# Two weight tiles at a time in layer two's dense products, and five layouts of split weight tiles

## The chip, the core and the metric

The kernel runs on one core of a Trainium2 chip. Its time is the device time of one execution in microseconds (us). TensorE multiplies, VectorE and ScalarE do elementwise work, GpSimd a little of it, and SyncE issues the transfers from HBM to the on-chip memory SBUF. In the profile these engines are PE (matrix products), PEld (the loads of PE's stationary operand, which overlap the products), DVE, ACT, POOL and SP. Three runs of the kernel before gave a median of 2337.14 us (2336.44 to 2337.54).

## The reference

The program is two layers of an encoder. A layer projects the residual stream with one wide matrix, runs gated linear attention and neighbourhood attention, projects back, adds and normalises, and then runs a squared-ReLU MLP with another normalisation:

```python
for l in range(DEPTH):                                   # DEPTH = 2
    proj = h @ w_in[l]                                   # 2048 -> 6176 columns
    mix  = concat(gla(proj), na(proj)) @ w_out[l]        # 2048 -> 2048
    h    = layer_norm(ALPHA * h + mix)
    ff   = square(relu(h @ w_ff1[l])) @ w_ff2[l]         # 2048 -> 8192 -> 2048
    h    = layer_norm(ALPHA * h + ff)
return h[:, 16:]                                         # the 16 meta tokens are dropped
```

There are 272 positions: 256 tokens and 16 meta tokens. Everything is float32. In layer two the meta tokens' results are needed only as keys and values, so most of that layer's products have 256 columns and not 272.

## The kernel before

**Three products for one.** Activations and weights are held as a high part and a low part (`x = h + l`, `w = wh + wl`, each in the type float32r), and a product is the sum of `wh*h`, `wh*l` and `wl*h`. A weight tile of 128 partitions x 1024 columns holds eight stationary blocks of 128x128. SP fetches it as `raw` (L189), ACT casts it to the high part `wh` (L212), DVE subtracts to get the low part `wl` (L213). `raw`, `wh` and `wl` have three buffers each, so a tile may be split when the tile three before it is used up.

**The layout of a split tile.** `wh` and `wl` are 1280 columns wide, so the eight blocks need not lie side by side. `blocks` takes three numbers: where the first block lies, how far the second block of a pair lies behind the first, and how far the next pair lies behind this one. Before, two sets of numbers exist: one for tiles whose products run in the short form below (high: 24, P, 2P; low: 8, P+32, 2P+64, with P = 128), and one for all the others (high: 0, P, 2P; low: 0, P+16, 2P+64). All numbers are float32 columns, 4 bytes each.

**The products of a tile.** `by_m` makes one output tile of 128 rows after another; each sums over `nk` blocks, eight to a weight tile, and calls `eight` for each weight tile. `eight` (its product is L247) issues PE's products in an order that a string gives: `h` is high weights times high activations, `l` high weights times low activations, `w` low weights times high activations. The long form, `hlhlww...`, has 24 products of up to 274 columns. The short form, `hwhw...`, is used where a product has 256 columns: the high and the low part of an activation lie close enough for one `h` product of 512 columns to do `wh*h` and `wh*l`, into the two halves of a PSUM bank; `w` is a product of 256 columns into the second half. An evict adds the halves.

**Dense and pitched activations.** In a dense activation tile the two parts of 256 columns lie side by side, and an `h` product streams 512 columns in one piece. The attention's outputs `y` and the MLP's inner activations `u` of layer two are dense, and so is `x` after layer two's first normalisation. Where `x` still has 272 positions (layer two's first projection) the parts are 288 columns apart, so that `h` streams two pieces of 256; these are called pitched here.

**What runs when.** Layer one uses the long form with 272 columns throughout. Where the normalisation is still being finished, the first two groups of a matrix run with two columns more (274 in layer one's MLP and in layer two's first projection, 258 in layer two's MLP), so that a product also gives two sums that the late correction needs. Layer two's short-form products are: 20 output tiles pitched in the first projection, then dense 12 output tiles of the output projection, 52 of the MLP's first matrix, and 31 of 32 of its second (whose `nk` is 32). `by_k` (L273) does the first group of some matrices, four output tiles at once.

**What sets the order.** Each engine takes its instructions in the order of its list. The lists follow the order in which the code issues, apart from a few places where the framework moves a product ahead because it expects another one's operand to be late. `weights` keeps one split tile ahead of the one in use; `pump` lets background generators (normalisation, attention) issue a step between tiles.

Of the kernel before, what the change touches and what calls it, by code (L numbers as in the profile page):

```python
# [14 lines left out]
P = 128  # L15
D = 2048
DC = D // P
T = 256
# [8 lines left out]
WB = 1024  # L27
# [11 lines left out]
PAD = 40  # L39
PITCH = 288  # L40
WIDE = 1280
HIGHS = {True: 24, False: 0}
LOWS = {True: (8, P + 32, 2 * P + 64), False: (0, P + 16, 2 * P + 64)}
TURNS = {True: "hwhwhwhwhwhwhwhw", False: "hlhlwwhlhlwwhlhlwwhlhlww"}


class Pair(tuple):


    def __new__(cls, both, dense=False):  # L50
        flat = both.rearrange("p a c -> p (a c)")
        parts = (flat[:, :T], flat[:, T:2 * T]) if dense else (both[:, 0, :], both[:, 1, :])
        made = super().__new__(cls, parts)
        made.both, made.once = both, flat[:, :2 * T] if dense else both[:, :, :T]
        return made


class Trunk:
    def __init__(self, ctx, tc, ins, out):
        self.ctx, self.tc, self.nc = ctx, tc, tc.nc  # L60
        self.i, self.out = ins, out
        self.bg, self.fg, self.credit, self.fcredit = deque(), deque(), 0, 0
        self.wants, self.due, self.late = {}, None, 0
        self.x = [None] * DC
        self.stream, self.ready = self.order(), deque()
        pool = lambda name, **k: ctx.enter_context(tc.tile_pool(name=name, **k))
        self.cp = pool("const", bufs=1)
        self.xp = pool("xhl", bufs=1)
        self.yp = pool("yhl", bufs=1)
        self.wp = pool("wst", bufs=3)  # L70
        self.jp = pool("jn", bufs=1)
        self.pm = pool("pm", bufs=4, space=PSUM)
        self.pb = pool("pb", bufs=4, space=PSUM)
# [80 lines left out]
    def order(self):  # L154

        i, first = self.i, [(), (WB // 2, WB)]
        for l in range(DEPTH):
            last = l + 1 == DEPTH
            na = [last and c % 3 == 0 for c in range(24)]
            groups = [(i["win"][l, g], [last and g in (3, 4, 5)] * 4 if g < 6 else na[4 * g - 24:4 * g - 20]) for g in range(12)]  # L160
            groups += [(i["wout"][l, g], [last and g > 0] * 4) for g in range(4)]
            for half in range(2):
                groups += [(i["wff1"][l, 8 * half + g], [last and (half > 0 or g > 2)] * 4) for g in range(8)]
                groups += [(i["wff2"][l, half, g], [last] * 4) for g in range(4)]
            if l == 0:
                for t in range(groups[0][0].shape[0]):
                    for w, _ in groups[:2]:
                        yield w[t], first.pop(0) if first else (WB,), False
                groups = groups[2:]
            for w, once in groups:  # L170
                n = w.shape[0]
                for t in range(n):
                    yield w[t], (WB,), once[4 * t // n]

    def weights(self):

        while len(self.ready) < 2:
            self.ready.append(self.made(*next(self.stream, (None, (), False))))
        return self.ready.popleft()

    def made(self, ap, ends, once):
        if ap is None:
            return None
        nc = self.nc
        raw = self.wp.tile([P, WB], F32, name="raw", tag="raw")
        wh, wl = (self.wp.tile([P, WIDE], F32R, name=nm, tag=nm) for nm in ("wh", "wl"))
        wh, wl = self.blocks(wh, HIGHS[once], P, 2 * P), self.blocks(wl, *LOWS[once])
        for c in map(slice, (0,) + ends, ends):
            nc.sync.dma_start(raw[:, c], ap[:, c])  # L189
            self.halves(raw[:, c], wh, wl, slice(c.start // P, c.stop // P))  # L190
        if not ends:
            self.head(ap, raw, wh, wl)
        return wh, wl
# [21 lines left out]
    def head(self, ap, raw, wh, wl):  # L215

        nc, q = self.nc, WB // 4
        both = self.xr.tile([P, 2, q + L], F32, name="head", tag="head", bufs=1)
        self.x[:2] = [self.pair(self.xp, "x", c) for c in range(2)]
        for c in range(2):  # L220
            nc.sync.dma_start(both[:, c], self.i["head"][:, c])
        nc.sync.dma_start(raw[:, 2 * q:], ap[:, 2 * q:])
        for c in range(2):
            at = slice(2 * c, 2 * c + 2)
            h, lo = (t[:, :L] for t in self.x[c])
            acts = lambda: self.split(both[:, c, q:], h, lo)
            weights = lambda: self.halves(both[:, c, :q], wh, wl, at)
            for f in (weights, acts) if c else (acts, weights):
                f()
        for at in (slice(4, 6), slice(6, 8)):  # L230
            self.halves(raw[:, at.start * P:at.stop * P], wh, wl, at)

    def eight(self, ps, wh, wl, x, n, first, last, once):
# [6 lines left out]
        for i, kind in enumerate(TURNS[once]):  # L240
# [5 lines left out]
                rhs, o = (v.once, ps) if kind == "h" else (v[0][:, :T], ps[:, T:])  # L246
            mm(o, lhsT=self.block(w, j), rhs=rhs, start=first and not i, stop=last and i == len(TURNS[once]) - 1)  # L247

    def whole(self, parts):

        if len(parts) == 1:
            return parts[0]
        t = self.jp.tile([P, T], F32, name="jn", tag="jn")
        self.nc.scalar.copy(t, parts[1])
        self.nc.vector.tensor_tensor(t, t, parts[0], ALU.add)
        return t
# [20 lines left out]
    def by_m(self, acts, ns, evict, pump=(0, 0), apart=False, renew=False, slim=()):  # L277

        nk = len(acts)
        for m, n in enumerate(ns):  # L280
            once = n == T and m not in slim
            ps = self.pm.tile([P, 512], F32, name="mm", tag="mm")
            for k in range(0, nk, 8):
                wh, wl = self.weights()
                self.eight(ps, wh, wl, acts[k:k + 8], n, not k, k == nk - 8, once)
                if k < nk - 8:
                    self.pump(*pump)
                if renew and m == len(ns) - 1 and not k:
                    self.renew(2)
            parts = [ps[:, :T], ps[:, T:]] if once else [ps[:, :n]]  # L290
            evict(m, parts if apart else self.whole(parts))
            self.pump(*pump)
# [916 lines left out]
```

## Time and profile before

| what | us |
|---|---|
| median of three runs | 2337.14 |
| the profiled execution | 2336.72 |
| its span, first to last instruction | 2334.9 |
| PE busy | 2326.3 |
| PEld busy (overlaps PE) | 2216.0 |
| DVE busy | 1527.4 |
| ACT busy | 1211.8 |
| POOL busy | 129.4 |

The profiled execution takes 1.8 us more than its span. PE is busy almost all the time, at a granted clock of 0.999. The traffic is 419 MB, nearly all of it the weights. A row of the timeline gives the start and the recorded duration of an instruction, or of several equal ones that follow each other; a product's recorded duration is longer than the time until the next product starts, because products are pipelined.

### The profile page before, as it was taken

How to read it: one execution, taken by the hardware profiler on the slowest of the kernel's cores; microseconds unless marked ns; L12 is line 12 of the kernel's file. 1: busy time of each engine (PE TensorE's matmuls, PEld its weight loads, DVE VectorE, ACT ScalarE, POOL GpSimd, SP SyncE). 2: the span in 40 equal slices, each digit the busy share in tenths (PEclk: the TensorE clock that was granted, in tenths of full speed). 3: DMA queues.
4: the chain of work that ended last, by engine and by line, in shares of the span. 5: the costliest groups of instructions: out<-in, count | busy, mean ns of one | idle time of the engine just before them, and what ended most of it. 6: DMA issues, size and time to landing. Idle time of an engine off the chain costs nothing.

```text
span 2334.9 us, 44618 instructions
## 1 busy us (share of the span) xinstructions
PE 2326.3 (100%) x18180; PEld 2216.0 (95%) x18180; DVE 1527.4 (65%) x2432; ACT 1211.8 (52%) x2100; POOL 129.4 (6%) x200
## 2 busy tenths in 40 slices
PE   9999999999999999999999999999999999999998
PEld 9999999999999999999999899989988888888888
DVE  5588777775544455546576887778766555666655
ACT  5666664564433344444456666655654334445443
POOL 0021110110000000000020111100100000000000
PEclk9999999999999999999999999999999999999999
DMA  8555545566666666665555555556666666667664
GB/s 264 154 163 154 152 140 178 173 179 181 179 182 178 180 179 181 181 181 177 178 183 168 172 163 158 162 158 189 191 191 193 193 190 191 193 193 221 190 191 151
DMA packets 118301, 419.02 MB, mean 179 GB/s; under 512 B 13512, under 2 KB 14024, under 8 KB 118096
## 3 DMA queue, kind: packets, MB, share of 16 engines
q1 hardware_dynamic: 117808, 415.65, 59.4%
q8 instruction: 142, 2.33, 0.4%
q14 instruction: 63, 0.52, 0.1%
q10 hardware_dynamic: 288, 0.52, 0.1%
HBM read 414.03 MB, written 2.10 MB: 178 GB/s over the span
## 4 chain that ended last, share of the span: by engine, by line
PE 98%; DVE 1%; issue 0%; ACT 0%; DVEq 0%; ACTq 0%
PE mm L247 86%; PE mm L273 6%; PE bg L273 1%; PE bg L784 1%; PE mm L723 1%; PE bg L584 1%; DVE wl L213 0%; PE bg L430 0%; PE mm L749 0%; DVE acc L1012 0%; PE mm L473 0%; PE bg L635 0%; PE bg L910 0%; PE bg L665 0%; PE bg L639 0%
## 5 line engine op out<-in xcount | busy, mean ns | idle before, releaser
L213 DVE TENSOR_TENSOR wl<-raw,wh 128x1024 fp32r<-128x1024 f32 (+1 forms) x770 | 942.9, 1225 | 637.8 <-ACT wh L212 631.8
L212 ACT CAST wh<-raw 128x1024 fp32r<-128x1024 f32 (+1 forms) x770 | 804.5, 1046 | 889.1 <-PE mm L247 703.0
L247 PE MATMUL mm<-x,wh 128*128 128x272 f32 (+3 forms) x5376 | 1094.3, 309 | 0.0
L247 PEld LDWEIGHTS mm<-x,wh 128*128 128x128 f32 x5376 | 803.7, 188 | 48.1 <-PE mm L723 0.6
L247 PE MATMUL mm<-x,wl 128*128 128x272 f32 (+3 forms) x3264 | 752.7, 283 | 0.0
L247 PEld LDWEIGHTS mm<-x,wl 128*128 128x128 f32 x3264 | 547.5, 188 | 0.0
L247 PE MATMUL mm<-y,wh 128*128 128x272 f32 (+2 forms) x2128 | 472.9, 319 | 0.0
L247 PEld LDWEIGHTS mm<-y,wh 128*128 128x128 f32 x2128 | 328.6, 188 | 26.9
L247 PE MATMUL mm<-u,wh 128*128 128x272 f32 (+2 forms) x1552 | 343.7, 318 | 0.0
L247 PE MATMUL mm<-y,wl 128*128 128x272 f32 (+1 forms) x1408 | 337.9, 282 | 0.7 <-DVE wl L213 0.7
L247 PEld LDWEIGHTS mm<-u,wh 128*128 128x128 f32 x1552 | 239.4, 188 | 19.5
L247 PE MATMUL mm<-u,wl 128*128 128x272 f32 (+1 forms) x1024 | 245.6, 282 | 0.0
L247 PEld LDWEIGHTS mm<-y,wl 128*128 128x128 f32 x1408 | 241.7, 188 | 1.4 <-DVE wl L213 1.1
L247 PEld LDWEIGHTS mm<-u,wl 128*128 128x128 f32 x1024 | 175.6, 188 | 0.0
L273 PE MATMUL mm<-x,wh 128*128 128x272 f32 (+1 forms) x512 | 83.8, 287 | 0.0
L273 PEld LDWEIGHTS mm<-x,wh 128*128 128x128 f32 x512 | 71.7, 191 | 0.0
L1000 POOL TENSOR_SCALAR acc<-acc,vec 128x272 f32<-128x272 f32 (+1 forms) x24 | 41.9, 1751 | 273.3 <-DVE acc L1012 155.3
L561 ACT COPY U<-S 128x272 f32<-128x272 f32 (+1 forms) x104 | 40.7, 429 | 23.2 <-DVE S L570 20.5
L273 PE MATMUL mm<-x,wl 128*128 128x272 f32 (+1 forms) x256 | 52.1, 286 | 0.5 <-DVE wl L213 0.5
L872 DVE TENSOR_TENSOR acc<-acc,mm 128x256 f32<-128x256 f32 (+1 forms) x71 | 30.3, 426 | 29.6 <-PE mm L247 29.1
L570 DVE TENSOR_TENSOR S<-S,dec 128x272 f32<-128x272 f32 (+1 forms) x112 | 46.3, 443 | 3.5 <-ACT U L561 2.5
L295 ACT CAST u<-ft 128x272 fp32r<-128x272 f32 (+1 forms) x64 | 26.2, 410 | 41.8 <-DVE ft L828 41.7
(265 smaller groups left out, 1647.5 us busy)
## 6 DMA issues: line engine op xcount, KB each, us to landing
raw<-in_wff SPq DMA_DIRECT2D x512, 512.0 KB, 3.8
raw<-in_win SPq DMA_DIRECT2D x190, 512.0 KB, 3.7
raw<-in_wout SPq DMA_DIRECT2D x64, 512.0 KB, 3.7
nb<-in_nab SPq DMA_DIRECT2D x16, 352.0 KB, 4.4
xraw<-in_xT SPq DMA_DIRECT2D x7, 272.0 KB, 5.9
out<-out SPq DMA_DIRECT2D x5, 256.0 KB, 3.1
brow<-in_norm SPq DMA_DIRECT2D x4, 256.0 KB, 4.5
gw<-in_wup SPq DMA_DIRECT2D x4, 196.0 KB
```

The costliest lines, as they stand in the source:

```text
L212: self.nc.scalar.copy(h, r)
L213: self.wl = self.nc.vector.tensor_tensor(lo, r, h.bitcast(F32), ALU.subtract).ins
L247: mm(o, lhsT=self.block(w, j), rhs=rhs, start=first and not i, stop=last and i == len(TURNS[once]) - 1)
L273: self.nc.tensor.matmul(ps[g + m][:, :n], lhsT=self.block(parts[p][0], 4 * j + m if first else 2 * m + j), rhs=acts[k + j][parts[p][1]][:, ...
L295: self.nc.scalar.copy(hi, src)
L561: nc.scalar.copy(U[:, lv % 4, j, :w].rearrange("p (n t h) -> p n t h", t=2, h=hb), bass.AP(S.tensor, S.offset + 2 * j * L, [S.ap[0], [2 * ...
L570: tt(o, o, totals(lv, odd, w), ALU.mult)
L584: nc.tensor.matmul(ps[b * 32:b * 32 + 32, o:o + w], lhsT=k[:, c:c + 32], rhs=q[:, r:r + w], start=True, stop=True)
L723: nc.tensor.matmul(ps[hh][:, t * NKEY:t * NKEY + NKEY], lhsT=q[hs, NM + t * P:NM + t * P + P], rhs=k[hs, t, :], start=True, stop=True)
L784: nc.tensor.matmul(po[t][hs, :P], lhsT=v2[ts, hs] if rest else v1[:, t, hs], rhs=p2[ts, hh, :] if rest else p1[:, 2 * hh + t, :], start=re ...
L872: tt(a, a, part, ALU.add)
L1000: nc.gpsimd.tensor_scalar(a, a, gain, bias, ALU.mult, ALU.add)
```

## The change

Three things change, and all else stays: every engine issues as many instructions as before.

- `by_m` takes 16 blocks a step where the output is in the short form and the activations are dense, and calls the new function `sixteen`. It takes two weight tiles, issues the 16 `h` products of both and then the 16 `w` products of both; the next call does `w` first and then `h`, the one after that `h` first again. So, over two calls, 16 `h`, 32 `w`, 16 `h`, and again. Between the two halves of a call it pumps once.
- The pitched tiles keep `eight` and the order `hwhw...`.
- The two sets of layout numbers become five. `once` (dense short form): high blocks start at 0 and not at 24, low ones at 16 and not at 8. `two` (pitched short form): high at 0, low (16, P+16, 2P+64). `all` is the old set of the long form. `all2` (274 columns): the second low block of a pair 32 columns further. `own2` (258 columns): the second high block of a pair 48 columns further in pairs of 2P+64, the second low one 16 further.

```diff
-HIGHS = {True: 24, False: 0}
...
+HIGHS = {"once": (0, P, 2 * P), "two": (0, P, 2 * P), "all": (0, P, 2 * P), "all2": (0, P, 2 * P), "own2": (0, P + 48, 2 * P + 64)}
...
@@ made
-        wh, wl = self.blocks(wh, HIGHS[once], P, 2 * P), self.blocks(wl, *LOWS[once])
+        wh, wl = self.blocks(wh, *HIGHS[kind]), self.blocks(wl, *LOWS[kind])
...
+    def sixteen(self, ps, x, first, last, pump):
+        both = [self.weights() for _ in range(2)]
+        self.low = not self.low
+        for i, low in enumerate((self.low, not self.low)):
+            for j, v in enumerate(x):
+                o, rhs = (ps[:, T:], v[0][:, :T]) if low else (ps, v.once)
+                self.nc.tensor.matmul(o, lhsT=self.block(both[j // 8][low], j % 8), rhs=rhs, start=first and not i + j,
+                                      stop=bool(last and i and j == 15), skip_group_check=True)
+            if not i:
+                self.pump(*pump)
...
@@ by_m
-            for k in range(0, nk, 8):
-                wh, wl = self.weights()
-                self.eight(ps, wh, wl, acts[k:k + 8], n, not k, k == nk - 8, once)
-                if k < nk - 8:
+            step = 16 if once and acts[0].dense else 8
+            for k in range(0, nk, step):
+                if step > 8:
+                    self.sixteen(ps, acts[k:k + 16], not k, k == nk - 16, pump)
+                else:
+                    wh, wl = self.weights()
+                    self.eight(ps, wh, wl, acts[k:k + 8], n, not k, k == nk - 8, once)
+                if k < nk - step:
                     self.pump(*pump)
```

The first place is PE's list in the MLP's second matrix of layer two, inside one output tile (`mm_22056`), at its second weight tile. Before, a high and a low product of the same activation tile alternate:

```order
L247 MATMUL mm_22056<-y6_19979,wh_22033 128x512
L247 MATMUL mm_22056<-y6_19979,wl_22034 128x256
L247 MATMUL mm_22056<-y7_19980,wh_22033 128x512
L247 MATMUL mm_22056<-y7_19980,wl_22034 128x256
L247 MATMUL mm_22056<-y8_19981,wh_22058 128x512
L247 MATMUL mm_22056<-y8_19981,wl_22059 128x256
```

The same output tile after, where the 16 high products of two weight tiles end and the 16 low ones begin:

```order
L264 MATMUL mm_22056<-y14_19987,wh_22058 128x512
L264 MATMUL mm_22056<-y15_19988,wh_22058 128x512
L264 MATMUL mm_22056<-y0_19973,wl_22018 128x256
L264 MATMUL mm_22056<-y1_19974,wl_22018 128x256
L264 MATMUL mm_22056<-y2_19975,wl_22018 128x256
L264 MATMUL mm_22056<-y3_19976,wl_22018 128x256
```

The low products have moved behind 16 high ones, so a product is now followed by one of its own kind, and the low part of a weight tile is used up later than its high part.

The second place is DVE's list around the same output tile; `wl_...` are low parts of weight tiles, the rows that read `mm_...` are evicts. Before:

```order
L213 TENSOR_TENSOR wl_22034<-raw_22032,wh_22033 128x8x128
L213 TENSOR_TENSOR wl_22059<-raw_22057,wh_22058 128x8x128
L848 TENSOR_SCALAR acc_18598<-acc_18598,mm_21965 128x256
L850 TENSOR_TENSOR acc_18598<-acc_18598,mm_21965 128x256
L213 TENSOR_TENSOR wl_22081<-raw_22079,wh_22080 128x8x128
L213 TENSOR_TENSOR wl_22103<-raw_22101,wh_22102 128x8x128
L213 TENSOR_TENSOR wl_22125<-raw_22123,wh_22124 128x8x128
```

After:

```order
L218 TENSOR_TENSOR wl_22018<-raw_22016,wh_22017 128x8x128
L218 TENSOR_TENSOR wl_22059<-raw_22057,wh_22058 128x8x128
L872 TENSOR_SCALAR acc_18598<-acc_18598,mm_21965 128x256
L874 TENSOR_TENSOR acc_18598<-acc_18598,mm_21965 128x256
L218 TENSOR_TENSOR wl_22065<-raw_22063,wh_22064 128x8x128
L218 TENSOR_TENSOR wl_22103<-raw_22101,wh_22102 128x8x128
L218 TENSOR_TENSOR wl_22109<-raw_22107,wh_22108 128x8x128
```

DVE's order is the same; what has moved is the moment at which PE gives it the buffer of a low part. `wl_22103` is made into the buffer of `wl_22018`, which PE has used up in the middle of the run of low products, and PE wants `wl_22103` itself as the last quarter of that run of 32.

More of the change, by code (lines that the diff above doesn't have):

```diff
@@ L41 @@
 WIDE = 1280
-HIGHS = {True: 24, False: 0}
-LOWS = {True: (8, P + 32, 2 * P + 64), False: (0, P + 16, 2 * P + 64)}
+HIGHS = {"once": (0, P, 2 * P), "two": (0, P, 2 * P), "all": (0, P, 2 * P), "all2": (0, P, 2 * P), "own2": (0, P + 48, 2 * P + 64)}
+LOWS = {"once": (16, P + 32, 2 * P + 64), "two": (16, P + 16, 2 * P + 64), "all": (0, P + 16, 2 * P + 64),
+        "all2": (0, P + 48, 2 * P + 64), "own2": (0, P + 32, 2 * P + 64)}
 TURNS = {True: "hwhwhwhwhwhwhwhw", False: "hlhlwwhlhlwwhlhlwwhlhlww"}
@@ L53, in __new__ @@
         made = super().__new__(cls, parts)
-        made.both, made.once = both, flat[:, :2 * T] if dense else both[:, :, :T]
+        made.dense, made.both, made.once = dense, both, flat[:, :2 * T] if dense else both[:, :, :T]
         return made
@@ L62, in __init__ @@
         self.bg, self.fg, self.credit, self.fcredit = deque(), deque(), 0, 0
-        self.wants, self.due, self.late = {}, None, 0
+        self.wants, self.due, self.late, self.low = {}, None, 0, True
         self.x = [None] * DC
@@ L158, in order @@
             last = l + 1 == DEPTH
-            na = [last and c % 3 == 0 for c in range(24)]
-            groups = [(i["win"][l, g], [last and g in (3, 4, 5)] * 4 if g < 6 else na[4 * g - 24:4 * g - 20]) for g in range(12)]
-            groups += [(i["wout"][l, g], [last and g > 0] * 4) for g in range(4)]
+            kind = lambda short, name: name if last and short else "all"
+            na = [kind(c % 3 == 0, "two") for c in range(24)]
+            groups = [(i["win"][l, g], [kind(g in (3, 4, 5), "two")] * 4 if g < 6 else na[4 * g - 24:4 * g - 20]) for g in range(12)]
+            if last:
+                groups[0] = groups[0][0], ["all2"] * 4
+            groups += [(i["wout"][l, g], [kind(g > 0, "once")] * 4) for g in range(4)]
             for half in range(2):
-                groups += [(i["wff1"][l, 8 * half + g], [last and (half > 0 or g > 2)] * 4) for g in range(8)]
-                groups += [(i["wff2"][l, half, g], [last] * 4) for g in range(4)]
+                groups += [(i["wff1"][l, 8 * half + g], [kind(half > 0 or g > 2, "once") if half or g > 1 else ("all2", "own2")[last]] * 4)
+                           for g in range(8)]
+                groups += [(i["wff2"][l, half, g], [kind(True, "once")] * 4) for g in range(4)]
             if l == 0:
@@ L167, in order, with made @@
                     for w, _ in groups[:2]:
-                        yield w[t], first.pop(0) if first else (WB,), False
+                        yield w[t], first.pop(0) if first else (WB,), "all"
                 groups = groups[2:]
-            for w, once in groups:
+            for w, kinds in groups:
                 n = w.shape[0]
                 for t in range(n):
-                    yield w[t], (WB,), once[4 * t // n]
+                    yield w[t], (WB,), kinds[4 * t // n]
     def weights(self):
         while len(self.ready) < 2:
-            self.ready.append(self.made(*next(self.stream, (None, (), False))))
+            self.ready.append(self.made(*next(self.stream, (None, (), None))))
         return self.ready.popleft()
-    def made(self, ap, ends, once):
+    def made(self, ap, ends, kind):
         if ap is None:
```

## The prediction

> **What bounds the kernel now.** The page comes first: the busy rows, the clock row and the chain.
>
> ```profile
> PE 2326.3 (100%) x18180; PEld 2216.0 (95%) x18180; DVE 1527.4 (65%) x2432; ACT 1211.8 (52%) x2100; POOL 129.4 (6%) x200
> ...
> PEclk9999999999999999999999999999999999999999
> ...
> PE 98%; DVE 1%; issue 0%; ACT 0%; DVEq 0%; ACTq 0%
> ```
>
> PE is busy throughout at full clock and makes 98% of the chain. The waits of PE say that nobody keeps it waiting:
>
> ```profile
> PE mm L247 <- DVE wl L213: 0.7, 1, 0.7
> PE mm L273 <- DVE wl L213: 0.5, 1, 0.5
> ```
>
> So the time is the number of products times their pace, and the change leaves the number alone. What matters is the pace, next whether DVE's low parts still come in time. The timeline of a dense stretch in the MLP shows the pace (first and last row of 16 high products and the 15 low ones between them):
>
> ```profile
> 1700.22 0.39 PE L247 MATMUL mm<-x,wh 128*128 128x512 f32 x1
> ...
> 1705.37 0.39 PE L247 MATMUL mm<-x,wh 128*128 128x512 f32 x1
> ```
>
> 5.15 us for 15 pairs is 343 ns a pair. The groups by form give recorded durations:
>
> ```profile
> L247 PE MATMUL mm<-x,wh 128*128 128x272 f32 x3584 | 588.5, 286 | 0.0
> L247 PE MATMUL mm<-x,wh 128*128 128x512 f32 x1152 | 400.2, 392 | 0.0
> ...
> L247 PE MATMUL mm<-x,wl 128*128 128x256 f32 x1152 | 321.8, 279 | 0.0
> L247 PE MATMUL mm<-y,wh 128*128 128x512 f32 x688 | 237.9, 389 | 0.0
> ...
> L247 PE MATMUL mm<-y,wl 128*128 128x256 f32 x704 | 194.7, 279 | 0.7 <-DVE wl L213 0.7
> L247 PE MATMUL mm<-u,wh 128*128 128x512 f32 x496 | 171.7, 389 | 0.0
> ...
> L247 PE MATMUL mm<-u,wl 128*128 128x256 f32 x512 | 141.5, 279 | 0.0
> ...
> L247 PE MATMUL mm<-x,wh 128*128 128x274 f32 x384 | 64.4, 290 | 0.0
> ...
> L247 PE MATMUL mm<-x,wh 128*128 128x258 f32 x256 | 41.4, 284 | 0.0
> L247 PE MATMUL mm<-x,wl 128*128 128x274 f32 x192 | 39.9, 288 | 0.0
> ...
> L247 PE MATMUL mm<-x,wl 128*128 128x258 f32 x128 | 26.0, 284 | 0.0
> ...
> L247 PE MATMUL mm<-u,wh 128*128 128x256 f32 x32 | 5.1, 280 | 0.0
> ```
>
> A high product of 512 columns records 389 and a low one 279, together 668, while the pair takes 343. A recorded duration therefore holds some 162 ns that overlap the next product ((668-343)/2), and pace is recorded less 162: high 227, low 117. The dense pairs are 832 (x) + 688 (y) + 496 (u) = 2016, worth 692 us; 320 of the 1152 x pairs are pitched.
>
> **The change part by part. Dense high products.** 2016 high products come in runs now. From 272 columns (286-162 = 124) to 512 (227) a column costs 0.43 ns; 512 columns are then 220.5, and 6 ns are left that another order might hide. That is the lower end, -6. The upper end is in three places of the old list where two high products do follow each other, in the output projection:
>
> ```profile
> 1567.08 0.63 PE L247 MATMUL mm<-y,wh 128*128 128x512 f32 x2
> 1567.55 0.28 PE L247 MATMUL mm<-y,wl 128*128 128x256 f32 x1
> ```
>
> Two took 0.47 us, 235 each and not 227: +8. These products lie at the old offset 24, and in a stretch where DVE and ACT disturb the pace, so they are weak evidence for runs at offset 0; but they are the only high-after-high rows of 512 columns. I take 0, the 389 of every dense row.
>
> **Dense low products.** In one stretch of the MLP the low rows have a spread, and the high ones none:
>
> ```profile
> L247 PE MATMUL mm<-u,wh x160: 389/389/389, 1865.0 to 1969.1; 128*128 128x512 f32 x160
> L247 PE MATMUL mm<-u,wl x160: 277/279/280, 1865.2 to 1969.3; 128*128 128x256 f32 x160
> ```
>
> The three numbers are minimum, median and maximum; low products stand at 277 or 280. The order, the columns and the activations are the same for all, so the 3 ns must come from where blocks lie; and the change moves all of them (low from 8 to 16, high from 24 to 0) and puts the load of another low block under a low product. Lower end: all at 277, -1.5 on average. Upper end: the one output tile of 256-column products that follow each other without a 512 between them stands at 280 (last row of the groups), and the nearest low group of the other loop, at the old long-form layout, at 282:
>
> ```profile
> L273 PE MATMUL mm<-y,wl 128*128 128x256 f32 x64 | 12.8, 282 | 0.0
> ```
>
> That is +1 to +3. I take -1.5, because half the products have it already: 2016 x 1.5 = -3.0 us. This is the weakest step, and the rivals start from it.
>
> The Trainium skill, "TensorE: Matmul & The Clock Gate", section "Back-to-back issue gap", puts a warm product at its columns over 2.4 GHz plus about 2.5 ns. By it a pair would be 215.8 + 109.2 = 325 ns, an estimate, and the rows show 343. By that page 18 ns of each pair would be loss, up to 37 us in all; by the row, the sum above stands.
>
> **Pitched pairs.**
>
> ```profile
> 1273.16 0.40 PE L247 MATMUL mm<-x,wh 128*128 128x512 f32 x1
> ...
> 1274.58 0.40 PE L247 MATMUL mm<-x,wh 128*128 128x512 f32 x1
> ```
>
> Four pairs take 1.42 us, 355 each, 12 more than dense ones. Only offsets change. Ends: down to the dense pace (320 x -12 = -3.8 us), up by 8 as in the high-after-high rows (+2.6). I take a third of the gain, -4 x 320 = -1.3 us.
>
> **274 and 258 columns.** 576 products of 274 columns pace at 290-162 = 128 and 288-162 = 126, against 124 for 272, whose two columns fewer are worth 1 ns. Only every second low block moves, so two of six transitions can change. Ends: down to 125 throughout (-2.5 x 576 = -1.4 us), up as much. I take -0.5. The 384 products of 258 columns pace at 122, the 256-column rows at 118; ends -3 x 384 = -1.2 and +1.2; I take -0.6.
>
> **Loads, DVE and buffers.** Nothing is added on DVE, ACT or SP, but the moment of release moves. Its price, from a dense stretch:
>
> ```profile
> 1900.38 0.39 PE L247 MATMUL mm<-u,wh 128*128 128x512 f32 x1
> ...
> 1900.73 0.39 PE L247 MATMUL mm<-u,wh 128*128 128x512 f32 x1
> 1900.81 1.05 ACT L212 CAST wh<-raw 128x1024 fp32r<-128x1024 f32 x1 [1.70 <-PE mm L247]
> ...
> 1901.89 1.23 DVE L213 TENSOR_TENSOR wl<-raw,wh 128x1024 fp32r<-128x1024 f32 x1 [1.52 <-ACT wh L212]
> ```
>
> The last high product of a tile starts at 1900.38 and records 0.39, so it ends at 1900.77; ACT starts 0.04 later, runs 1.05, and DVE follows 0.03 after it for 1.23. Put on the new order, with a run of four low parts a, b, c, d of 8 x 0.117 = 0.94 us each: d goes into a's buffer. a's last product ends 0.16 after b begins, DVE starts 0.04 later and is done at 0.20 + 1.23 = 1.43 after b began; d is wanted at 1.87, its load some 0.12 before that. The margin is 0.3 us, if DVE has nothing else to do just then. In DVE's list c's subtraction and one evict remainder at most stand just before d's in the MLP, and both have their inputs long before; the next evict stands behind. High parts have more: d's high buffer is free 3.6 us before d's low part is wanted. So no wait, at a price of 2 us per 0.03 us if the margin fails in each of some 63 such runs. What hides it is PE's run of b and c.
>
> Transfers follow DVE: `raw` is free once its low part is made. They come in twos now, but the mean rate is the same, one of 512 KB per 2.75 us (8 x 343 ns), so I count nothing for them.
>
> **Start of the dense stretch.** The output projection is where DVE is most loaded, and PE once waits:
>
> ```profile
> 1547.00:1614.00 67.00, 66.34 (x385) 58.06 (x384) 59.29 (x122) 35.98 (x56) 0.00 (x0) 1.00 0.63 188
> ...
> 1560.57 0.65 PE L247 MATMUL mm<-y,wh 128*128 128x512 f32 x2
> 1561.89 0.38 PE L247 MATMUL mm<-y,wl 128*128 128x256 f32 x1 [0.66 <-DVE wl L213]
> ```
>
> DVE (fourth number after the window, 59.29) works 88% of these 67 us. The two products should take 0.47 and took 1.32: 0.85 lost. 16 high products first (3.6 us) give DVE time, 16 low ones first take it away. Ends: -0.85 and +3; I take -0.8.
>
> **Sum:** -3.0 - 1.3 - 0.5 - 0.6 - 0.8 = -6.2 us on the profiled execution's 2336.72 (span 2334.9 and 1.8 around it; 0.4 under the median of the runs): 2330.5.
>
> **The rivals.**
>
> *Runs cost more (slower).* High products after high ones at 231, half of the +8 above, and low ones at 280 (+1): 2016 x 5 = +10.1, less 3.2 for the other terms: 2343.6; with the whole +8, 2352. For it: the rows of 0.47 us for two, and the 280 and 282. Against: they lie at other offsets. From +1.6 ns a pair on it eats the other gains, from +4 on the kernel is slower by 0.2%. Chance 0.25.
>
> *DVE comes late (slower).* d's subtraction misses by 0.25 us in each run: 63 x 0.25 = +15.8, with the gains 2346; in the output projection alone, +3. For it: a margin of 0.3 that any extra step on DVE eats. Against: the list as built. Chance 0.05, counted as slower.
>
> *Nothing moves.* The dense pace stays at 343, since under each product there is one load of 128 columns as before, and the layouts give 1 to 3 us: 2335. For it: high rows at 389 wherever their neighbours lie. Chance 0.22. The same page of the Trainium skill, section "LDWEIGHTS (loading the stationary operand)", gives a load as columns over 1.2 GHz, 107 ns for 128 by that figure, whatever precedes it: by that rule a low product is held by its load in either order, and the pair keeps its pace.
>
> *A run hides the overhead.* High products at 221: 2016 x 6 = -12, with the rest 2318. For it only the 0.43 ns a column. Chance 0.08; the 37 us of the page above lie beyond it, and no row reaches there.
>
> **How the numbers follow.** 0.2%, about what a measurement of this kernel can tell from no change, is 4.7 us. The forecast (0.40) and the hidden overhead are faster: 0.48. Nothing moves: 0.22. Dearer runs and a late DVE: 0.30. The range 2316 to 2351 takes in the hidden overhead and dearer runs nearly to their whole +8; the forecast's own is 2324 to 2333.
>
> **What would show it.** In the groups by form of the profile after: dense high products still at 389 and low ones at 277 to 278 bear the forecast out; high at 393 or more, or low at 280 and more, is the slower rival; high near 383 the faster one. Pitched high rows, with x kept apart by form, should fall from some 12 above dense ones; 274 and 258 from 290 and 284. PE's waits for DVE's low parts should stay under 1 us in all; more than 5 there, spread over the MLP, is the late DVE. The prediction is wrong at once if high-after-high at offset 0 differs from 389 by more than 2 ns, since 2016 products multiply it.

## The result: 2332.08 us, and where 4.7 us went

The changed kernel takes 2332.08 us (median of 15 runs, 2330.84 to 2333.74) against 2336.83 (median of 15 beside it): a ratio of 0.9979, with a 95% interval of 0.9973 to 0.9986. It is faster, since the interval lies below 1, and by about the 0.2% that the prediction took as the least that can be told. The profiled execution took 2332.43 us with a span of 2330.6.

The page of the changed kernel, its busy row and its chain by engine:

```profile
PE 2319.4 (100%) x18180; PEld 2208.1 (95%) x18180; DVE 1519.6 (65%) x2432; ACT 1221.6 (52%) x2100; POOL 129.4 (6%) x200
...
PE 97%; DVE 2%; ACT 1%; issue 0%; DMA 0%; SPq 0%; DVEq 0%; ACTq 0%
```

PE still bounds the kernel with the same 18180 products. Its groups by form (count | busy us, mean recorded ns | idle before) answer those shown of before; L264 is the product of `sixteen`, L252 that of `eight`:

```profile
L252 PE MATMUL mm<-x,wh 128*128 128x272 f32 x3584 | 588.6, 286 | 0.5 <-ACT ft L484 0.5
...
L264 PE MATMUL mm<-x,wh 128*128 128x512 f32 x832 | 193.8, 390 | 0.0
L264 PE MATMUL mm<-y,wh 128*128 128x512 f32 x688 | 162.9, 390 | 2.0 <-ACT wh L217 2.0
...
L264 PE MATMUL mm<-u,wh 128*128 128x512 f32 x496 | 118.3, 390 | 0.0
L252 PE MATMUL mm<-x,wh 128*128 128x512 f32 x320 | 112.7, 396 | 0.0
...
L264 PE MATMUL mm<-x,wl 128*128 128x256 f32 x832 | 98.8, 276 | 0.0
...
L264 PE MATMUL mm<-y,wl 128*128 128x256 f32 x688 | 84.9, 276 | 0.0
L252 PE MATMUL mm<-x,wh 128*128 128x274 f32 x384 | 63.8, 289 | 0.0
...
L264 PE MATMUL mm<-u,wl 128*128 128x256 f32 x496 | 61.8, 277 | 0.0
L252 PE MATMUL mm<-x,wh 128*128 128x258 f32 x256 | 40.8, 281 | 0.0
L252 PE MATMUL mm<-x,wl 128*128 128x274 f32 x192 | 40.1, 290 | 0.0
L252 PE MATMUL mm<-x,wl 128*128 128x258 f32 x128 | 25.6, 281 | 0.0
```

Layer one's 272 columns are as before. Dense low products fell from 279 to 276 or 277, dense high ones rose from 389 to 390, 258 columns fell from 284 to 281, 274 columns hardly moved. The timeline of a dense stretch shows two calls of `sixteen`, high first and low first; rows are merged runs, so the distance between two starts is the time of a run:

```profile
1897.73 3.81 PE L264 MATMUL mm<-u,wh 128*128 128x512 f32 x16
1901.39 3.79 PE L264 MATMUL mm<-y,wh 128*128 128x512 f32 x16
1905.01 1.98 PE L264 MATMUL mm<-y,wl 128*128 128x256 f32 x16
1906.83 1.98 PE L264 MATMUL mm<-u,wl 128*128 128x256 f32 x16
1908.65 3.82 PE L264 MATMUL mm<-u,wh 128*128 128x512 f32 x16
```

32 pairs take 1908.65 - 1897.73 = 10.92 us, 341 ns a pair and not 343. By stretch of the program, from the starts of the same output tiles in both traces (profiled executions, us):

| stretch | before | after | difference |
|---|---|---|---|
| up to the first pitched tile | 1272.1 | 1272.7 | +0.6 |
| pitched tiles and the long-form tiles between them | 249.1 | 247.7 | -1.4 |
| output projection, dense part | 67.6 | 68.6 | +1.0 |
| 258 columns | 47.0 | 46.2 | -0.8 |
| MLP, dense part | 626.8 | 623.1 | -3.7 |

The first row holds 0.3 us gained on 274 columns and a wait of a transition between two loops that comes and goes with the execution. The output projection lost. The waits of PE have a new row:

```profile
PE mm L264 <- ACT wh L217: 2.0, 2, 1.8
```

### The profile page after: what moved, and what is told of

Same layout as the page of the kernel before. It is cut to its first block, busy times and chain, and to the rows that moved or that the text cites. A ratio compares the mean times of both kernels' runs of the same rounds, so it can differ in the third digit from the quotient of the medians.

```text
span 2330.6 us, 44637 instructions
## 1 busy us (share of the span) xinstructions
PE 2319.4 (100%) x18180; PEld 2208.1 (95%) x18180; DVE 1519.6 (65%) x2432; ACT 1221.6 (52%) x2100; POOL 129.4 (6%) x200
## 4 chain that ended last, share of the span: by engine, by line
PE 97%; DVE 2%; ACT 1%; issue 0%; DMA 0%; SPq 0%; DVEq 0%; ACTq 0%
PE mm L252 57%; PE mm L264 29%; PE mm L293 6%; PE bg L293 1%; PE bg L808 1%; PE mm L747 1%; PE bg L608 1%; DVE wl L218 1%; PE bg L454 0%; ACT wh L217 0%; PE mm L773 0%; DVE acc L1036 0%; DMA raw<-in_win 0%; PE bg L934 0%; PE mm L497 0%
## 5 line engine op out<-in xcount | busy, mean ns | idle before, releaser
L252 PE MATMUL mm<-x,wh 128*128 128x272 f32 (+3 forms) x4544 | 805.7, 294 | 0.5 <-ACT ft L484 0.5
L252 PEld LDWEIGHTS mm<-x,wh 128*128 128x128 f32 x4544 | 646.7, 188 | 15.6 <-ACT ft L484 0.7
L252 PE MATMUL mm<-x,wl 128*128 128x272 f32 (+3 forms) x2432 | 519.6, 284 | 0.0
L252 PEld LDWEIGHTS mm<-x,wl 128*128 128x128 f32 x2432 | 390.8, 188 | 0.0
L252 PE MATMUL mm<-y,wh 128*128 128x272 f32 (+1 forms) x1440 | 235.0, 285 | 0.0
L252 PEld LDWEIGHTS mm<-y,wh 128*128 128x128 f32 x1440 | 199.7, 188 | 0.1
L264 PE MATMUL mm<-x,wh 128*128 128x512 f32 x832 | 193.8, 390 | 0.0
L264 PEld LDWEIGHTS mm<-x,wh 128*128 128x128 f32 x832 | 154.2, 188 | 31.0
L252 PE MATMUL mm<-u,wh 128*128 128x272 f32 (+1 forms) x1056 | 172.1, 285 | 0.0
L264 PE MATMUL mm<-y,wh 128*128 128x512 f32 x688 | 162.9, 390 | 2.0 <-ACT wh L217 2.0
L264 PEld LDWEIGHTS mm<-y,wh 128*128 128x128 f32 x688 | 128.6, 188 | 28.7 <-ACT wh L217 2.4
L252 PE MATMUL mm<-y,wl 128*128 128x272 f32 (+1 forms) x720 | 146.4, 284 | 0.0
L252 PEld LDWEIGHTS mm<-u,wh 128*128 128x128 f32 x1056 | 146.3, 188 | 0.0
L264 PE MATMUL mm<-u,wh 128*128 128x512 f32 x496 | 118.3, 390 | 0.0
L252 PEld LDWEIGHTS mm<-y,wl 128*128 128x128 f32 x720 | 112.6, 188 | 0.0
L264 PEld LDWEIGHTS mm<-u,wh 128*128 128x128 f32 x496 | 90.9, 188 | 17.7
L252 PE MATMUL mm<-u,wl 128*128 128x272 f32 (+1 forms) x528 | 107.3, 284 | 0.0
L264 PEld LDWEIGHTS mm<-x,wl 128*128 128x128 f32 x832 | 98.4, 188 | 2.0
L264 PE MATMUL mm<-x,wl 128*128 128x256 f32 x832 | 98.8, 276 | 0.0
L264 PEld LDWEIGHTS mm<-y,wl 128*128 128x128 f32 x688 | 84.2, 188 | 2.9
```

The lines of the kernel that those rows point to most:

```text
L264: self.nc.tensor.matmul(o, lhsT=self.block(both[j // 8][low], j % 8), rhs=rhs, start=first and not i + j, stop=bool(last and i and j == 15 ...
```

## The experiments

Two theories came out of the result. By the first, the run is the cause: a low product that follows a low one is cheap, wherever the blocks lie. By the second, the layout is the cause: it is the offsets, in any order. The first four kernels take the change apart.

### The order without the layouts

```diff
-HIGHS = {"once": (0, P, 2 * P), "two": (0, P, 2 * P), ...
+HIGHS = {"once": (24, P, 2 * P), "two": (24, P, 2 * P), ...
-LOWS = {"once": (16, P + 32, 2 * P + 64), ...
+LOWS = {"once": (8, P + 32, 2 * P + 64), ...
```

The lines are cut short. `two` is back at the old numbers of the short form too, and `all2` and `own2` are those of the long form again.

> The new order of dense products with the old numbers of every layout (high blocks from 24, low ones from 8 and 40 in turn). If the run is the cause (a low product followed by a low one is cheap wherever the blocks lie), low products of 256 columns record 276 to 277 and high ones 389 to 390, as in the changed kernel, and the time lacks only the side layouts' 1.6 us: 2333.5 to 2334.5 us. If the layout is the cause, low products in runs record 279 to 280, high ones more than 390, and the time is 2337 to 2341 us.

It took 2354.7 us, 1.0076 of the kernel before (1.0059 to 1.0093): slower by 18 us, beyond what either theory gave. The products that read `u` in a stretch of the MLP (recorded ns, minimum/median/maximum), first of the changed kernel, then of this one:

```profile
L264 PE MATMUL mm<-u,wl x160: 276/276/278, 1863.2 to 1963.1; 128*128 128x256 f32 x160
L264 PE MATMUL mm<-u,wh x160: 389/389/398, 1865.0 to 1966.6; 128*128 128x512 f32 x160
```

```profile
L264 PE MATMUL mm<-u,wl x176: 277/280/283, 1860.8 to 1975.2; 128*128 128x256 f32 x176
L264 PE MATMUL mm<-u,wh x176: 391/396/400, 1862.7 to 1978.8; 128*128 128x512 f32 x176
```

Runs at the old offsets make high products 7 ns dearer than they were in the kernel before, and low ones 1 ns.

### The layouts without the order

```diff
-            step = 16 if once and acts[0].dense else 8
+            step = 8
```

> The five new layouts with the old alternating order hwhw in the dense tiles. If the run is the cause, dense low products stay at 279 and high ones at 389, the output projection keeps the old kernel's pace, and the time is 2335 us (side layouts alone). If the layout is the cause, low products record 276 in this order too and the time is 2329 to 2330 us, better than the changed kernel, since the output projection does not lose its 1 us.

2348.6 us, 1.0051 (1.0036 to 1.0066). The same rows:

```profile
L252 PE MATMUL mm<-u,wl x168: 278/280/281, 1859.8 to 1974.3; 128*128 128x256 f32 x168
L252 PE MATMUL mm<-u,wh x167: 392/397/397, 1859.9 to 1974.0; 128*128 128x512 f32 x167
```

Both theories fall. Each half of the change alone costs 12 to 18 us; only together do they gain. Of the two orders and the two sets of offsets, the old order wants the old offsets and the new order the new ones. This gives a third theory: a product's pace is set by where the block lies that is loaded under it, and by the order in which such blocks come; in a run it is its own kind's block.

### Shorter runs, one tile at a time

```diff
-        for i, kind in enumerate(TURNS[once]):
+        for i, kind in enumerate("hhhhhhhhwwwwwwww" if runs else TURNS[once]):
```

with `step = 8` and `runs` set for dense tiles in the short form.

> One weight tile at a time, eight high products and then eight low ones, new layouts. If an own-kind neighbour is what makes a product cheap, 14 of 16 transitions have it: low products 276 to 277, the dense stretch of the MLP within 1 us of the changed kernel's, the output projection at most as late as the old one's; time 2331.5 to 2333 us. If it takes runs over two tiles, the low products record 278 to 279 and the time is 2335 us.

2335.0 us, 0.9993 (0.9984 to 1.0002): no change that can be told. The rows:

```profile
L252 PE MATMUL mm<-u,wh x160: 388/391/398, 1861.6 to 1965.1; 128*128 128x512 f32 x160
L252 PE MATMUL mm<-u,wl x160: 276/276/279, 1863.4 to 1966.1; 128*128 128x256 f32 x160
```

Low products are as cheap as in long runs, high ones are not, and the MLP's dense part takes 628.2 us, 5.1 more than in the changed kernel, where at most 1 was expected: the loss is on the other kind. Where it sits shows when the distances between the starts of successive products are averaged by place in the run (dense part of the MLP, distances of 400 ns and more left out as waits; worked out from the starts in the traces):

```
place in the run            1      2      3      4      5      6 and on
changed kernel, high ns   232.5  235.6  228.5  232.3  230.8    226.7
runs of 8,      high ns   232.5  235.8  228.6  232.5  230.8    226.7
runs of 8,      low ns    117.5  115.8  114.2  113.3  113.3    113.3
```

After a change of kind the pace needs five high or three low products to settle, then it stays at 226.7 and 113.3, in runs of 8 as in the changed kernel's. A change to high costs 26 ns and one to low 8, 34 for both. The alternating kernel paid 226.7 and 116.7. In the MLP's 1824 pairs, 340 ns each when settled, the sums of what lies above that agree: 228 runs of 8 pay 7.6 us, 57 reversed pairs of calls in the changed kernel pay 2.0, and the alternating kernel paid 6.2.

### The order without the reversal

```diff
-        self.low = not self.low
+        self.low = False
```

> Two tiles together, high first in every call, so runs of 16 high and 16 low. If the reversal matters for the pace, twice as many changes of kind cost over 1 us; if not, the MLP's dense stretch is within 0.3 us of the changed kernel's. The margin of the low part that is made into the buffer just used up is larger here (a run of high products lies between), so a loss in the output projection that comes from that margin shrinks: 2331 to 2332 us. If that loss comes from DVE's load alone, it stays: 2332 us.

2331.4 us, 0.9978 (0.9969 to 0.9987), and two effects that cancel: the MLP's dense part takes 624.8 us, 1.7 more than the changed kernel, and the output projection 66.2, 2.4 less. 114 changes to high and 114 to low instead of 57 each are 57 x 34 ns = 1.9 us, which is what the reversal is worth in the MLP. The output projection shows it as PE's idle time. Windows over its dense part (its length, then busy time and count of PE, PEld, DVE, ACT, POOL, then granted clock, DMA share and GB/s), of the changed kernel and of this one:

```profile
1545.50:1614.10 68.60, 66.59 (x389) 58.25 (x388) 59.15 (x124) 36.69 (x56) 0.00 (x0) 1.00 0.58 183
```

```profile
1545.50:1611.70 66.20, 66.20 (x389) 58.19 (x388) 59.07 (x124) 37.60 (x57) 0.00 (x0) 1.00 0.62 190
```

PE sat idle for 2.0 us with the reversal and not at all without. DVE has the same 59 us of work in both. In the changed kernel's timeline PE stops at a high tile whose cast has not been made:

```profile
1564.18 1.04 ACT L217 CAST wh<-raw 128x1024 fp32r<-128x1024 f32 x1 [2.83 <-DVE acc L896]
1565.28 1.68 PE L264 MATMUL mm<-y,wh 128*128 128x512 f32 x6 [1.84 <-ACT wh L217]
```

Without the reversal the same cast comes no sooner, but PE is then in the middle of 16 high products:

```profile
1562.43 3.81 PE L264 MATMUL mm<-y,wh 128*128 128x512 f32 x16
1564.23 1.05 ACT L217 CAST wh<-raw 128x1024 fp32r<-128x1024 f32 x1 [2.90 <-DVE acc L896]
```

So this cast is made no later with the reversal; it is wanted earlier. The view names an evict of DVE as what the cast waited for, but the cast does not read it. Its tile's transfer was issued at 1560.41 in the changed kernel, when a subtraction of DVE had given a buffer of `raw` free, and it had landed at 1564.08 by the semaphore that the cast waits for. The chain is thus DVE's subtraction, the transfer, the cast and PE.

### One offset at a time

The third theory has a sharp test: put back the old offset of one kind alone.

```diff
-LOWS = {"once": (16, P + 32, 2 * P + 64), ...
+LOWS = {"once": (8, P + 32, 2 * P + 64), ...
```

> The changed kernel with its dense low blocks back at 8 and 40, its high blocks at 0. Theory: a product's pace is set by where the block lies that is loaded under it, in a run its own kind's. Then in runs of the MLP the high products keep 226.7 ns once settled, the low ones take some 118 instead of 113.3, and the time is 2016 x 4.7 = 9.5 us over the changed kernel's, 2341 to 2342 us. Rival: high and low offsets must fit each other, and both kinds lose: high ones 230 or more, 2350 us.

One time, 2340.87 us, just under the forecast.

```profile
L264 PE MATMUL mm<-u,wh x161: 387/389/398, 1859.6 to 1970.4; 128*128 128x512 f32 x161
L264 PE MATMUL mm<-u,wl x160: 277/280/284, 1865.4 to 1966.9; 128*128 128x256 f32 x160
```

And the high one:

```diff
-HIGHS = {"once": (0, P, 2 * P), ...
+HIGHS = {"once": (24, P, 2 * P), ...
```

> The changed kernel with its dense high blocks back at 24, its low blocks at 16 and 48. Theory: low products in runs keep 113.3 to 113.6 ns, high ones take 231 to 237, mean 234, and the time is 2016 x 7 = 14 us over the changed kernel's, 2345 to 2347 us. Rival (offsets must fit each other): low ones lose as well, 117 or more, and the time is 2353 us.

One time, 2344.34 us, a little under the forecast.

```profile
L264 PE MATMUL mm<-u,wh x167: 392/397/400, 1859.8 to 1972.5; 128*128 128x512 f32 x167
L264 PE MATMUL mm<-u,wl x160: 276/276/278, 1867.0 to 1968.9; 128*128 128x256 f32 x160
```

In each, the kind whose blocks were moved back is dear (by the starts in the MLP, low products 117.9 ns on average in the first, high ones 234.1 in the second) and the other keeps its pace once settled. One side effect: with low blocks from 8 the high runs need ten products to settle and not five.

That inside a run the pace is that of its own kind's offset is shown. That it goes by the block loaded under a product, as the theory says, is not: in a run the product's own block and the loaded one are of the same kind. Where they differ, place alone does not give the pace. In runs of 8 and 16 at the new offsets the last high product, with the low block at 16 next, takes 225.8 ns. In the alternating order at the same offsets (the layouts without the order) a high product takes 229.2 and 235.8 in turn, and the one of 229.2 also has a low block next that lies at 16. (Offsets are counted from the last multiple of 64 columns, so that low blocks lie at 16 and 48 in turn.) So what went before counts as well, and why 0, 16 and 48 suit runs and 24, 8 and 40 suit alternation stays open.

### Runs of four

```diff
-        for i, kind in enumerate(TURNS[once]):
+        for i, kind in enumerate("hhhhwwwwhhhhwwww" if runs else TURNS[once]):
```

with `step` and `runs` as in the kernel with runs of 8.

> One weight tile at a time in the order hhhhwwwwhhhhwwww, new layouts. Theory: after each change of kind some products pay before the pace settles (in the runs of 8, 16 and 32 alike 5.8, 8.9, 1.8, 5.7 and 4.1 ns for the first five high ones, 4.1, 2.6 and 0.9 for the first three low ones). Runs of 4 then never settle: four pairs cost 4 x 340 + 30 = 1390 ns, 347.5 a pair against 343.3 in the alternating order, and the time is 2342 to 2345 us. Rival: the offset at a change is a matter of a new tile, not of the kind; then the second run of four in a tile costs nothing and the time is as with runs of 8, 2335 us.

One time, 2339.52 us, between the two forecasts. The MLP's dense part is at 632.8 us, 6.0 over the kernel before: 346.9 a pair, which is the settling cost (347.5 was expected; the fourth high product, followed by a low one, pays 2.5 and not 5.7). The rest of the distance to the forecast is the output projection, which took 67.1, 0.5 less than before, and the other layouts, which gave their 2 us. The second run of four in a tile pays like the first (232.5, 235.8, 228.4 and 229.1 ns against 232.5, 235.8, 228.3 and 229.2), so the cost is that of a change of kind and not of a tile.

```profile
L252 PE MATMUL mm<-u,wh x160: 389/394/398, 1863.5 to 1968.2; 128*128 128x512 f32 x160
L252 PE MATMUL mm<-u,wl x160: 277/278/279, 1864.4 to 1968.8; 128*128 128x256 f32 x160
```

### The reversal in the MLP only

```diff
-        self.low = not self.low
+        self.low = self.snake and not self.low
...
+            self.snake = False
...
+            self.snake = True
```

The two assignments stand ahead of the output projection's dense tiles and behind them.

> The changed kernel without the reversal in the output projection (high first in each of its 12 calls), with it in the MLP. If the output projection's loss comes from low products being wanted first while DVE is loaded, its stretch is 2.4 us shorter than the changed kernel's, as it was with the reversal left out everywhere, the MLP's dense stretch stays as short as the changed kernel's (3.7 us under the old one), and the time is 2329 to 2330 us, better than both. If the two interact, 2331 to 2332 us.

2330.51 us, 0.9974 of the kernel before (0.9965 to 0.9983): the lowest median of all, 1.6 us under the changed kernel's and half a us above the forecast. Its interval overlaps the changed kernel's, so the stretches say more than the total. The output projection takes 66.2 us as it did without the reversal, the MLP's dense part 623.5, 0.4 more than in the changed kernel; that 0.4 is single late products, and settling costs the same 2.0. Of the 2.0 us that PE waited for casts a tenth is left, and that one lies in the MLP (at 2146.2), none in the output projection:

```profile
PE mm L264 <- ACT wh L217: 0.2, 1, 0.2
```

## Why the prediction came out right, and which steps were wrong

The time lies in the range, 1.6 us over the predicted 2330.5, and on the forecast side. That it came so close is partly luck: dense low products gave some 6 us and not 3.0, and this paid for two things that the sum did not hold, the settling of high products (1.4 in the MLP) and the late products of the output projection (+1.5 where the sum had -0.8).

- **Dense high products, taken at 0.** Right to a first look: 390 against 389. Once settled, a high product takes 226.7 ns in runs as it did in alternation, so there were no 6 ns to hide (the 220.5 that they rest on comes out as 219.7 from its own two figures, which changes nothing). The mean rose from 226.7 to 227.5, 1.4 us in the MLP, by the settling after each change, which no term held.
- **Dense low products, taken at -1.5 ns.** Mis-sized by half: they fell by 3.1 on average, from 116.7 to 113.6 with five late products left out. That is -5.6 us in the MLP (0.5 of which the late ones took back) and -0.6 in the output projection. The lower end, "all at 277", was not low enough, since no row of before showed 113.3.
- **The reason given for it failed.** "The 3 ns must come from where blocks lie" took place alone for the cause. For the old order that holds as far as it goes: by their starts, low products there take 115.0 and some 118.5 ns in turn, as their blocks lie at 8 and at 40. But the 113.3 of the new order is under both. The layouts alone made low products 280 and high ones 397. Place matters only together with the order; a row of an alternating list, at whatever offset, could not price a run.
- **The dearer-runs rival** had a real price, at the offset its rows had: with blocks from 24, high after high costs 7 ns more, close to its +8. Its weak point was named, that those rows lie at another offset, and that decided.
- **Pitched pairs -1.3, 274 columns -0.5, 258 columns -0.6:** measured -1.4 for the pitched stretch, -0.3 and -0.8. Here the prediction said no more than that offsets change, and the kernel with the layouts alone gives the same paces.
- **DVE's margin of 0.3 us** held but for a few: in the MLP the last low tile of a run of 32 came late in 2 of 57 runs, by 0.2 us each.
- **Start of the dense stretch, -0.8:** the wrong sign. The stretch took 1.0 us more although its low products had gained 0.6. Late products cost 2.6 us there and not 1.1 as before, so the term itself measured +1.5. 16 high products first did help: without the reversal nothing is late and the stretch is 1.4 us shorter than before. But the term put that gain above the cost of low products first, which its own upper end of +3 had covered. Where DVE works 86 to 89% of the time (59 us of 66 to 69), wanting earlier what hangs on its results cost 2.4.
- **The pages.** By the figure of the Trainium skill, "TensorE: Matmul & The Clock Gate", section "Back-to-back issue gap", which the page gives for a single isolated product, 37 us lay in these pairs, an estimate. A settled pair takes 340.0 ns and not 325: of the 18 ns a pair, 3.4 could be had here, 2016 x 3.4 = 6.9 us of the 37. By the rule of the same page of the Trainium skill, section "LDWEIGHTS (loading the stationary operand)", as the prediction used it, a load costs its columns whatever precedes it and the pair keeps its pace. The traces disagree, since low products with the same load of 128 columns went at 113.3, 116.7 or 118 ns; and the page's 107 ns is less than the 117 of a low product, so that figure alone would not have held it.

## What to carry to other kernels

A tuned order and a tuned layout can be one setting: test them together, since here each half alone was slower by 12 to 18 us and both together faster by 4.7. Where products run back to back, look at the distance between starts by place in a run of equal products: it shows whether the pace is constant or is paid after each change. And an order that wants an operand earlier is free only where its maker has time, so it is to be chosen stage by stage.

## What the runs showed of the hardware

With the new offsets settled runs go at 226.7 ns for 512 columns and 113.3 for 256, at a granted clock of 0.999 to 1.0: twice, so these two widths leave no fixed part per product, and 0.443 ns a column. Moving the blocks changed the pace of a run: low ones by 8 columns (32 bytes) from 113.3 to 117.9 ns on average, high ones by 24 columns (96 bytes) from 226.7 to 234.1. After a change of kind it took five high or three low products to settle, the same in runs of 8, 16 and 32. What in the memory or in PE makes these patterns was not settled by any run here, and other offsets were not tried.
